# Where the stationary weights lie in their buffers: one fixed place for the seven-block chunks, eight places in turn for the plain ones

## The chip, the core and the metric

The kernel runs on one core of one Trainium2 chip. The metric is the device time of one execution in microseconds (us); a result is the median of several runs. In the profile, PE is the matrix engine (TensorE), PEld its weight loads, DVE, ACT and POOL are the vector, scalar and GpSimd engines, and SP issues most of the DMA transfers.

## What is computed

The reference is a two-layer encoder over 512 tokens of width 1024, all in float32. Layer 0 has two groups of attention heads side by side, layer 1 attention over a window of neighbours; each layer ends in a squared-ReLU network of inner width 4096. Cut to what matters here:

```python
for layer in range(DEPTH):                      # DEPTH = 2
    hn = rmsnorm(h, norm_mix[layer])
    if layer % 2 == 0:
        h = h + hybrid_attention(hn, ...)
    else:
        h = h + neighbourhood_attention(hn, w_qkv, rpb, w_out)
    hf = rmsnorm(h, norm_ffn[layer])
    u = jax.nn.relu(hf @ ffn_w_up[layer])       # 512x1024 @ 1024x4096
    h = h + (u * u) @ ffn_w_down[layer]         # 512x4096 @ 4096x1024
return rmsnorm(h, final_norm)
```

## The kernel before

**Three matmuls for one product.** Every float32 operand is held as a high part and a low part in the type `float32r`. A product of a weight block and an activation tile is three matmuls that add up in one PSUM bank: high weight with high activation, high weight with low activation, low weight with high activation. The weights are the stationary operand (a 128x128 block that PE loads before each matmul) and the activations the moving operand that streams through it.

**Weight chunks.** Weights come in chunks of up to 1024 columns. SP loads a chunk into a buffer; ACT copies it into a tile `whi` (three buffers of it), which rounds it to the high part; DVE subtracts this from the raw chunk and writes the rest to a tile `wlo` (four buffers). There are three generators for it:

- `chunk` (from L205): the plain one. ACT writes `whi` (L234, and DVE at L232 for the first), DVE writes `wlo` (L224).
- `summed_chunk` (from L248): also plain, but `wlo` is made by an ACT copy with the sign turned (L261) and a DMA that adds the raw weights to it (L263); ACT writes `whi` at L266.
- `seven_chunk` (from L362): for products that are done in seven block products instead of eight. A raw chunk holds a 2x2 arrangement of 128x128 blocks; three tensor-tensor operations, on POOL mostly (L372 to L374), make the sums and differences, ACT writes the seven blocks (896 columns) to `whi` (L379), DVE to `wlo` (L380).

A planner (`plan`, `weights`, `preload`, `begin`) keeps the list of all chunks in the order of use, loads up to five ahead and makes up to two ahead.

**The matmuls that use them.** `mm3` (L623 to L625) does the three matmuls of a plain block with moving tiles of 512 columns. `Seven.run` (L467 to L469) does the seven blocks of a seven-block chunk, three matmuls each, 21 in all, with moving tiles of 256 columns. The seven-block products stand in four runs, in each of which nothing else is on PE: 52 chunks in the first up projection, 32 in the first down projection, and 52 and 28 in the second ones: 164 chunks, 3444 matmuls. At L1728 to L1730 and L1058 to L1060 (256 columns) and L2038 to L2040 (512 columns) plain chunks are the moving operand instead.

**Places.** All activation slots and weight buffers start, in the built program, at the same remainder modulo 64 float32 columns (256 bytes), and within a slot the moving tiles start at multiples of 256 columns; the blocks of a weight tile start 128 columns apart. So what a weight tile has of its own is the number of columns from the start of its buffer, modulo 64. I call that number its **place**; place 0 is where the moving tiles lie. Before, plain chunks start at the start of their buffers and so have place 0 (but for a few blocks of other widths). Seven-block chunks go through `places()` (L355): number *i* puts its high part at column 8 (i mod 16) and its low part at a column that shifts against it every 16 chunks, so both parts go through the eight places 0, 8, 16, ... 56.

The order of the work is written out by hand; the tile framework adds the semaphores.

Of the kernel before, what the change touches and what calls it, by code (L numbers as in the profile page):

```python
# [9 lines left out]
F32R = mybir.dt.float32r  # L10
# [8 lines left out]
P = 128  # L19
# [11 lines left out]
def f32(ap):  # L31
    return ap.bitcast(F32)
# [3 lines left out]
def encoder_kernel(ctx: ExitStack, tc: tile.TileContext, ins, out, dbg=None):  # L36
# [5 lines left out]
    wp = ctx.enter_context(tc.tile_pool(name="wp", bufs=3))  # L42
# [19 lines left out]
    def nm(s):  # L62
        cnt[0] += 1
        return f"{s}_{cnt[0]}"
# [137 lines left out]
        return got[0]  # L202


    def chunk(parts, nk, ncol, heads=None, eng=None, first=False):  # L205

        raw = wp.tile([P, 1024], F32, tag="raw", bufs=4, name=nm("raw"))
        r3 = raw[:, 0 : nk * ncol].rearrange("p (k n) -> p k n", k=nk)
        for lo, n, src in parts:
            dst = r3[:, :, lo : lo + n]  # L210
            if len(src.shape) == 3:
                SP.dma_start(dst, src)
            else:
                for k in range(nk):
                    SP.dma_start(dst[:, k].rearrange("p (z m) -> p z m", z=src.shape[2]), src[:, k])
        yield
        hi = wp.tile([P, 1024], F32R, tag="whi", name=nm("whi"))
        lo_ = wp.tile([P, 1024], F32R, tag="wlo", bufs=4, name=nm("wlo"))
        m = nk * ncol
        v = lambda t: t[:, 0:m].rearrange("p (k n) -> p k n", k=nk)  # L220
        lows = []

        def low(to, src, high):
            z = lambda: (eng or DVE).tensor_tensor(to, src, f32(high), op=ALU.subtract)  # L224
            if eng:
                z()
            else:
                lows.append(z)

        if heads is None:  # L230
            if first:
                DVE.tensor_copy(hi[:, 0:m], raw[:, 0:m])  # L232
            else:
                ACT.activation(hi[:, 0:m], raw[:, 0:m], AF.Copy)  # L234
            low(lo_[:, 0:m], raw[:, 0:m], hi[:, 0:m])
        else:

            na, nb = heads
            hn = ncol // (na + nb)
            r4 = r3.rearrange("p k (h e) -> p k h e", h=hn)  # L240
            for e0, n, o in ((0, na, 0), (na, nb, hn * na)):
                z = [v(t)[:, :, o : o + hn * n].rearrange("p k (h e) -> p k h e", h=hn) for t in (hi, lo_)]
                src = r4[:, :, :, e0 : e0 + n]
                ACT.activation(z[0], src, AF.Copy)
                low(z[1], src, z[0])
        yield v(hi), v(lo_), lows

    def summed_chunk(parts, nk, ncol, heads=None, eng=None):  # L248

        raw = wp.tile([P, 1024], F32, tag="raw", bufs=4, name=nm("raw"))  # L250
        v = lambda t: t.rearrange("p (k n) -> p k n", k=nk)
        (o, n, src), = parts
        if len(src.shape) == 3:
            each = lambda t: [(v(t), src)]
        else:
            each = lambda t: [(v(t)[:, k].rearrange("p (z m) -> p z m", z=src.shape[2]), src[:, k]) for k in range(nk)]
        for d, x in each(raw):
            SP.dma_start(d, x)
        yield
        lo_ = wp.tile([P, 1024], F32R, tag="wlo", bufs=4, name=nm("wlo"))  # L260
        ACT.activation(lo_, raw, AF.Copy, scale=-1.0)  # L261
        for d, x in each(lo_):
            tc.keep_in_program_order(POOL.dma_start(d, x, accum_op=ALU.add))  # L263
        yield
        hi = wp.tile([P, 1024], F32R, tag="whi", name=nm("whi"))
        ACT.activation(hi, raw, AF.Copy)  # L266
        yield v(hi), v(lo_), []

    def rows(w, k0, nk):
        return w[k0 * P : (k0 + nk) * P, :].rearrange("(k p) n -> p k n", p=P)  # L270
# [6 lines left out]
    def plan(*spec, make=None):  # L277
        asked.append((make or chunk, spec))
        return len(asked) - 1
# [7 lines left out]
    def begin(i):  # L287
        while begun[0] < len(loaded):
            make = asked[begun[0]][0]
            if make is summed_chunk and begun[0] > i + SUM:  # L290
                break
            if make in (summed_chunk, seven_chunk):
                next(loaded[begun[0]])
            begun[0] += 1
# [55 lines left out]
    SEVEN = [(0, 0), (2, 2), (4, 5), (3, 3), (5, 4), (6, 1), (1, 6)]  # L350

    reserve = [3]
    place = [0]

    def places():  # L355

        i = place[0]
        place[0] += 1
        a = i % 16
        return 8 * a, 8 * ((a + (0, 1, 2, 4, 8, 3, 6, 12, 15, 14)[i // 16 % 10]) % 16)  # L360

    def seven_chunk(w, k0, c0, eng=None):  # L362


        slot = Slot(F32) if len(free) > reserve[0] else None
        raw = slot.t if slot else wp.tile([P, 1024], F32, tag="raw", bufs=4, name=nm("raw"))
        SP.dma_start(raw[:, 0:512].rearrange("p (k n) -> p k n", k=2), rows(w, k0, 2)[:, :, c0 : c0 + 256])
        r = raw.rearrange("p (b n) -> p b n", n=P)
        yield
        held = (lambda z: z) if eng else tc.keep_in_program_order  # L370
        eng = eng or POOL
        held(eng.tensor_tensor(r[:, 6], r[:, 0], r[:, 1], op=ALU.subtract))  # L372
        held(eng.tensor_tensor(r[:, 4:6], r[:, 2:3].to_broadcast([P, 2, P]), r[:, 0:7:6], op=ALU.add))  # L373
        held(eng.tensor_tensor(r[:, 7], r[:, 3], r[:, 5], op=ALU.subtract))  # L374
        yield
        a, b = places()
        hi = wp.tile([P, 1024], F32R, tag="whi", name=nm("whi"))[:, a : a + 896]
        lo = wp.tile([P, 1024], F32R, tag="wlo", bufs=4, name=nm("wlo"))[:, b : b + 896]
        ACT.activation(hi, raw[:, 128:1024], AF.Copy)  # L379
        DVE.tensor_tensor(lo, raw[:, 128:1024], f32(hi), op=ALU.subtract)  # L380
        if slot:
            slot.free()
        yield hi, lo, []

    class Seven:
# [63 lines left out]
        def plan(self, w, c0, pairs=None):  # L449

            return [plan(w, pairs[kp] if pairs else 2 * kp, c0, DVE if pairs and c0 and kp in (2, 5) else None,
                         make=seven_chunk)
                    for kp in range(self.np)]
# [86 lines left out]
    def product8(w, first, U, evac, eng=None):  # L540


        nk = len(U)
        ids = [plan([(0, D, rows(w, k, 1))], 1, D, None, eng, make=chunk if n < 2 else summed_chunk)
               for n, k in enumerate(first)]

# [340 lines left out]
    def load_w(k):  # L887
        w = rows(w_in, k, 1)
        W[k] = chunk([(0, 256, w[:, :, 512:768]), (256, 128, w[:, :, 0:128])], 1, 384, first=k == 0)
        next(W[k])  # L890
# [739 lines left out]
    def projC(t):  # L1630

        def ev(j, b):
# [34 lines left out]
            else:  # L1667
# [35 lines left out]
                def last():  # L1703
# [4 lines left out]
        return product(w_qkv, 0, XP, [(D * z + P * t, P) for z in range(2)], lambda j, b: ev(1 - j, b),  # L1708
                       lambda n: [mmb() for _ in range(n)], kstep=4, stride=D, order=(1, 0), nk=KD,
                       make=None if t else summed_chunk)  # L1710

    VC = {}
# [425 lines left out]
```

## Time and profile before

| what | value |
|---|---|
| median of 3 runs | 1150.22 us (1149.85 to 1150.63) |
| the profiled execution, own time | 1149.85 us |
| its span, first to last instruction | 1148.1 us |
| granted TensorE clock | 0.998 |
| PE busy | 1138.1 us, 99% of the span |
| DVE, ACT, POOL busy | 894.2, 669.3, 602.7 us |

The time of a matmul in the profile runs from its start to a modelled end and overlaps the next matmul. What counts for the time of the program is the **step**: from the start of one matmul to the start of the next. A view by windows gives it as the length of the window by the number of matmuls in it, less those that began before the window; the timeline gives it from starts, rounded to 0.01 us.

### The profile page before, as it was taken

The numbers are of one execution on the slowest core, as the hardware profiler recorded it, in microseconds if no ns is written. First come the engines' busy times: TensorE is split into PE (matmuls) and PEld (weight loads), VectorE is DVE, ScalarE is ACT, GpSimd is POOL, SyncE is SP. The second block draws the span as 40 slices with busy tenths as digits, with TensorE's granted clock in tenths as the row PEclk, the third lists the DMA queues.
The fourth block names the chain that finished last, engine by engine and source line by source line (L and its number), as shares of the span: only waits on it lengthen the run. The fifth ranks groups of instructions, "written<-read, shape, count | busy, mean of one in ns | idle before, by whom it ended". The sixth has DMA issues, their size and how long they took to land.

```text
span 1148.1 us, 20506 instructions
## 1 busy us (share of the span) xinstructions
PE 1138.1 (99%) x7348; PEld 1025.7 (89%) x7348; DVE 894.2 (78%) x1570; ACT 669.3 (58%) x1133; POOL 602.7 (52%) x722
## 2 busy tenths in 40 slices
PE   9999999999999999999999999999999999999997
PEld 8787888888899999899998998988889999989996
DVE  7887998988968777978775666667997777697874
ACT  6676785755346668534464556545553666773334
POOL 4456432327698993379432232231388889435740
PEclk9999999999999999999999999999999999999999
DMA  7322441222523235933585565333344232372332
GB/s 238 108 71 76 112 123 56 65 65 95 170 85 97 89 93 147 275 97 102 147 171 159 149 174 129 117 109 120 106 151 128 75 95 90 77 190 72 121 121 74
DMA packets 118325, 136.06 MB, mean 119 GB/s; under 512 B 9923, under 2 KB 99952, under 8 KB 118224
## 3 DMA queue, kind: packets, MB, share of 16 engines
q1 hardware_dynamic: 110736, 119.83, 34.4%
q0 software_dynamic: 7312, 14.83, 6.7%
q8 instruction: 58, 0.95, 0.4%
q14 instruction: 43, 0.35, 0.1%
q10 hardware_dynamic: 176, 0.10, 0.0%
HBM read 112.70 MB, written 6.29 MB: 104 GB/s over the span
## 4 chain that ended last, share of the span: by engine, by line
PE 92%; issue 3%; DVE 3%; ACT 1%; POOL 0%; DMA 0%; POOLq 0%; DVEq 0%; ACTq 0%
PE mm L623 9%; PE mm L624 8%; PE mm L625 8%; PE mm L468 4%; PE mm L467 4%; PE mm L469 4%; PE t L468 3%; PE t L469 3%; PE t L467 3%; PE s L1148 3%; PE o L1136 3%; PE s L467 2%; PE s L468 2%; PE s L469 2%; PE s L623 2%
## 5 line engine op out<-in xcount | busy, mean ns | idle before, releaser
L380 DVE TENSOR_TENSOR wlo<-a,whi 128x896 fp32r<-128x896 f32 x106 | 129.7, 1227 | 58.9 <-ACT whi L379 58.4
L623 PE MATMUL mm<-a,whi 128*128 128x512 f32 x428 | 172.7, 404 | 0.1
L624 PE MATMUL mm<-a,whi 128*128 128x512 f32 x428 | 167.9, 392 | 0.0
L625 PE MATMUL mm<-a,wlo 128*128 128x512 f32 x428 | 167.0, 391 | 0.0
L379 ACT ACTIVATE whi<-a 128x896 fp32r<-128x896 f32 x106 | 100.8, 951 | 111.8 <-PE s L468 28.5
L224 DVE TENSOR_TENSOR wlo<-raw,whi 128x1024 fp32r<-128x1024 f32 (+4 forms) x93 | 105.4, 1139 | 27.0 <-ACT whi L234 26.6
L234 ACT ACTIVATE whi<-raw 128x1024 fp32r<-128x1024 f32 (+3 forms) x96 | 88.2, 920 | 56.3 <-PE s L624 23.2
L468 PE MATMUL mm<-a,whi 128*128 128x256 f32 x430 | 120.8, 281 | 0.0
L469 PE MATMUL mm<-a,wlo 128*128 128x256 f32 x430 | 120.7, 281 | 0.0
L467 PE MATMUL mm<-a,whi 128*128 128x256 f32 x430 | 120.6, 281 | 0.0
L379 ACT ACTIVATE whi<-raw 128x896 fp32r<-128x896 f32 x58 | 55.1, 954 | 84.1 <-PE s L468 23.0
L373 POOL TENSOR_TENSOR a<-a 128x256 f32<-128x256 f32 x104 | 96.9, 932 | 8.2
L625 PEld LDWEIGHTS mm<-a,wlo 128*128 128x128 f32 x428 | 80.3, 188 | 17.1
L374 POOL TENSOR_TENSOR a<-a 128x128 f32<-128x128 f32 x104 | 90.5, 870 | 8.2
L1156 POOL TENSOR_SCALAR p<-p,ti 128x512 f32<-128x512 f32 x64 | 48.0, 751 | 88.4 <-DVE ti L1155 67.7
L623 PEld LDWEIGHTS mm<-a,whi 128*128 128x128 f32 x428 | 80.5, 188 | 15.5 <-issue 0.5
L624 PEld LDWEIGHTS mm<-a,whi 128*128 128x128 f32 x428 | 80.7, 189 | 13.5
L372 POOL TENSOR_TENSOR a<-a 128x128 f32<-128x128 f32 x104 | 77.2, 743 | 27.8 <-DMA a<-in_ffn_w_up_dram 23.1
L1785 POOL TENSOR_SCALAR p<-p,ti 128x256 f32<-128x256 f32 x64 | 35.6, 567 | 104.5 <-DVE ti L1784 91.6
L380 DVE TENSOR_TENSOR wlo<-raw,whi 128x896 fp32r<-128x896 f32 x58 | 71.0, 1235 | 24.6 <-ACT whi L379 24.5
L468 PE MATMUL t<-a,whi 128*128 128x256 f32 x312 | 87.5, 281 | 0.0
L469 PE MATMUL t<-a,wlo 128*128 128x256 f32 x312 | 87.5, 280 | 0.0
(449 smaller groups left out, 3618.8 us busy)
## 6 DMA issues: line engine op xcount, KB each, us to landing
a<-in_ffn_w_up_dram SPq DMA_DIRECT2D x102, 256.0 KB, 2.7
raw<-in_ffn_w_down_dram SPq DMA_DIRECT2D x34, 512.0 KB, 4.4
raw<-in_ffn_w_down_dram SPq DMA_DIRECT2D x56, 256.0 KB, 2.6
raw<-in_od_w_qkv_dram SPq DMA_DIRECT2D x64, 128.0 KB, 3.5
raw<-in_ffn_w_up_dram SPq DMA_DIRECT2D x12, 512.0 KB, 4.1
wlo<-in_ffn_w_down_dram POOLq DMA_DIRECT2D x12, 512.0 KB, 6.2
a<-a SPq DMA_DIRECT2D x17, 256.0 KB, 3.4
bx<-a SPq DMA_DIRECT2D x32, 128.0 KB, 5.4
```

The source lines that it names most:

```text
L224: z = lambda: (eng or DVE).tensor_tensor(to, src, f32(high), op=ALU.subtract)
L234: ACT.activation(hi[:, 0:m], raw[:, 0:m], AF.Copy)
L373: held(eng.tensor_tensor(r[:, 4:6], r[:, 2:3].to_broadcast([P, 2, P]), r[:, 0:7:6], op=ALU.add))
L374: held(eng.tensor_tensor(r[:, 7], r[:, 3], r[:, 5], op=ALU.subtract))
L379: ACT.activation(hi, raw[:, 128:1024], AF.Copy)
L380: DVE.tensor_tensor(lo, raw[:, 128:1024], f32(hi), op=ALU.subtract)
L467: PE.matmul(o, wh, x[:, 0], start=kp == 0 and n in (0, 1, 3, 5), stop=False, skip_group_check=True)
L468: PE.matmul(o, wh, x[:, 1], start=False, stop=False, skip_group_check=True)
L469: PE.matmul(o, wl, x[:, 0], start=False, stop=kp == self.np - 1, skip_group_check=True)
L623: PE.matmul(o, wh, xh, start=first, stop=False)
L624: PE.matmul(o, wh, xl, start=False, stop=False)
L625: PE.matmul(o, wl, xh, start=False, stop=last)
```

## The change

Seven-block chunks all get one place: both parts start at column 16 of their buffers. Plain chunks, of both generators, now go through `places()`: chunk *i* has its high part at column 8 (i mod 8) and its low part at 8 ((i mod 8 + i div 8) mod 8), so that every pair of the eight places 0 to 56 occurs in turn. To make room, `whi` and `wlo` buffers are 1088 columns wide instead of 1024 (a multiple of 64 again, so a place means the same as before). The order of the instructions on every engine, their sizes and what they wait for are the same as before.

```diff
+    place = [0]
+    def places():
+        i = place[0]
+        place[0] += 1
+        a = i % 8
+        return 8 * a, 8 * ((a + i // 8) % 8)
     def chunk(parts, nk, ncol, heads=None, eng=None, first=False):
...
-        hi = wp.tile([P, 1024], F32R, tag="whi", name=nm("whi"))
-        lo_ = wp.tile([P, 1024], F32R, tag="wlo", bufs=4, name=nm("wlo"))
+        a, b = places()
+        hi = wp.tile([P, 1088], F32R, tag="whi", name=nm("whi"))[:, a : a + 1024]
+        lo_ = wp.tile([P, 1088], F32R, tag="wlo", bufs=4, name=nm("wlo"))[:, b : b + 1024]
...
     def summed_chunk(parts, nk, ncol, heads=None, eng=None):
...
-        lo_ = wp.tile([P, 1024], F32R, tag="wlo", bufs=4, name=nm("wlo"))
+        a, b = places()
+        lo_ = wp.tile([P, 1088], F32R, tag="wlo", bufs=4, name=nm("wlo"))[:, b : b + 1024]
...
-        hi = wp.tile([P, 1024], F32R, tag="whi", name=nm("whi"))
+        hi = wp.tile([P, 1088], F32R, tag="whi", name=nm("whi"))[:, a : a + 1024]
...
-    place = [0]
-    def places():
-        i = place[0]
-        place[0] += 1
-        a = i % 16
-        return 8 * a, 8 * ((a + (0, 1, 2, 4, 8, 3, 6, 12, 15, 14)[i // 16 % 10]) % 16)
     def seven_chunk(w, k0, c0, eng=None):
...
-        a, b = places()
-        hi = wp.tile([P, 1024], F32R, tag="whi", name=nm("whi"))[:, a : a + 896]
-        lo = wp.tile([P, 1024], F32R, tag="wlo", bufs=4, name=nm("wlo"))[:, b : b + 896]
+        hi = wp.tile([P, 1088], F32R, tag="whi", name=nm("whi"))[:, 16:912]
+        lo = wp.tile([P, 1088], F32R, tag="wlo", bufs=4, name=nm("wlo"))[:, 16:912]
```

## The prediction

> **What bounds the kernel now.** I read the page's busy table and its chain first, then what PE waited for, then the matmuls' pace in the four runs of seven-block chunks.
>
> ```profile
> span 1148.1 us, 20506 instructions
> PE 1138.1 (99%) x7348; PEld 1025.7 (89%) x7348; DVE 894.2 (78%) x1570; ACT 669.3 (58%) x1133; POOL 602.7 (52%) x722
> PE 92%; issue 3%; DVE 3%; ACT 1%; POOL 0%; DMA 0%; POOLq 0%; DVEq 0%; ACTq 0%
> ```
>
> PE is busy for 99% of the span and the chain that ended last lies on it. The longest entry in the list of what PE waited for, and one of the shortest:
>
> ```profile
> PE o L158 <- POOL zeros L131: 1.0, 1, 1.0
> PE t L652 <- DVE rsB L722: 0.2, 1, 0.2
> ```
>
> So no wait is there to be won. The order of the instructions is unchanged, and the only way for this edit to move the time is the step from one matmul to the next. The windows view, one window inside each of the four seven-block runs (length, PE busy, number of matmuls):
>
> ```profile
> 319.00:447.00 128.00, 128.00 (x1086) 128.00 (x1086) 94.13 (x109) 83.04 (x104) 107.42 (x128) 1.00 0.29 86
> ...
> 491.00:570.00 79.00, 79.00 (x670) 79.00 (x669) 59.40 (x70) 33.97 (x40) 58.37 (x64) 1.00 0.36 116
> ...
> 873.00:1001.00 128.00, 128.00 (x1085) 128.00 (x1085) 93.78 (x108) 82.52 (x103) 106.71 (x127) 1.00 0.28 83
> ...
> 1046.00:1114.00 68.00, 68.00 (x578) 68.00 (x577) 53.50 (x65) 27.57 (x32) 44.22 (x50) 1.00 0.39 125
> ```
>
> A matmul here lasts 281 ns by the groups below, so each window also counts the 2.4 that began before it: 403 us / (3419 - 9.5) = **118.2 ns a step**. The whole-span windows view of L467 and of L624 gives their counts, 1148 and 703; times three, 3444 seven-block and 2109 plain matmuls:
>
> ```profile
> 0.00:1149.00 1149.00, 321.92 (x1148) 1.00 0.42 118
> ```
> ```profile
> 0.00:1149.00 1149.00, 274.84 (x703) 1.00 0.42 118
> ```
>
> **The seven-block chunks.** Before, they went through all places, so the trace already holds the place that they all get now. First and last of the 21 matmuls of four chunks, 20 steps between them: chunk 6 (both parts at column 48), chunk 10 (both at 80, which is place 16), chunk 64 (columns 0 and 64, place 0), chunk 66 (16 and 80, place 16).
>
> ```profile
> 333.38 0.28 PE L467 MATMUL s<-a,whi 128*128 128x256 f32 x1
> ...
> 335.73 0.28 PE L469 MATMUL o<-a,wlo 128*128 128x256 f32 x1
> ```
> ```profile
> 343.32 0.28 PE L467 MATMUL mm<-a,whi 128*128 128x256 f32 x1
> ...
> 345.59 0.28 PE L469 MATMUL s<-a,wlo 128*128 128x256 f32 x1
> ```
> ```profile
> 520.75 0.28 PE L467 MATMUL mm<-a,whi 128*128 128x256 f32 x1
> ...
> 523.14 0.28 PE L469 MATMUL s<-a,wlo 128*128 128x256 f32 x1
> ```
> ```profile
> 525.74 0.28 PE L467 MATMUL mm<-a,whi 128*128 128x256 f32 x1
> ...
> 528.01 0.28 PE L469 MATMUL s<-a,wlo 128*128 128x256 f32 x1
> ```
>
> 2.35 us / 20 = 117.5 ns; 2.27 / 20 = **113.5**; 2.39 / 20 = 119.5; 113.5 again. There are five chunks with both parts at place 16 (numbers 2, 10, 66, 74 and 162: the first up projection and both down projections are among them), and each takes this pace from its first matmul to its last; no chunk at another pair of places holds it throughout. The same shows in the mean time of a matmul: the page's group of L467, and the group of L467 inside chunk 10 alone.
>
> ```profile
> L467 PE MATMUL mm<-a,whi 128*128 128x256 f32 x430 | 120.6, 281 | 0.0
> ```
> ```profile
> L467 PE MATMUL mm<-a,whi 128*128 128x256 f32 x5 | 1.4, 276 | 0.0
> ```
>
> Since the wider buffers are again multiples of 64 columns, the change gives all 164 chunks these places: (118.2 - 113.5) x 3444 = **-16.2 us**, all of it on PE and so on the path. Bounds: -16.2 if all four runs fall into this pace, -2.4 (0.7 ns x 3444) if all keep the 117.5 of chunk 6. I take the full value: a run that has it is not disturbed, because no other matmul stands within a run and all chunks now have one place, while the five chunks of before had neighbours at other places and took the pace at once.
>
> One rule speaks against this. The Trainium skill, "SBUF — State Buffer", section "Who interferes with whom", gives PE a read port for the moving operand and an independent one for weight loads, and says that PE never waits on anyone. By it the place of a weight tile would not matter and the sum would be 1150. The rows of chunks 64 and 66, one after the other with the same instructions and 6 ns apart in the step, differ from it.
>
> **The plain chunks.** They leave place 0 and go through all pairs of places. The rows show place 0 alone. In the down projections, where 24 matmuls of a chunk follow each other undisturbed, its step is (all PE, two windows):
>
> ```profile
> 449.00:490.00 41.00, 41.00 (x182) 1.00 0.93 261
> 1004.00:1044.00 40.00, 40.00 (x179) 1.00 0.59 152
> ```
>
> With 1.7 matmuls of 389 ns begun before each, 81 us / 357.6 = 226.5 ns. This is twice 113.3, the undisturbed pace for twice the columns: place 0 is a good one for 512 columns once the pattern has settled. It is not always settled. Where other matmuls come between, the step is longer for some matmuls; a stretch of six at the same place 0:
>
> ```profile
> 50.06 0.39 PE L624 MATMUL mm<-a,whi 128*128 128x512 f32 x1
> ...
> 51.45 0.39 PE L624 MATMUL mm<-a,whi 128*128 128x512 f32 x1
> ```
>
> 1.39 us / 6 = 231.7 ns. Over all plain chunks the mean matmul of L624 lasts 274.84 / 703 = 391.0 ns, against 389 in the settled window:
>
> ```profile
> L624 PE MATMUL mm<-a,whi 128*128 128x512 f32 x15 | 5.8, 389 | 0.0
> ```
>
> so the mean step before is about 228.5. At other places, bounds from these rows: all 2109 settled, -2.0 ns or -4.2 us; none settled, +3.2 ns or +6.7 us; 6 ns above the settled step, as chunk 64 has it against chunk 66, 232.5 or +8.4 us. With 256 columns only one pair of places in 64 was seen to hold the best pace throughout, and a chunk of 24 matmuls has a new pair each time, so I take three quarters of the way to "none settled": **+5.0 us**.
>
> Where plain chunks are the moving operand (L1728 to L1730, 128 matmuls each), the mean is at place 0
>
> ```profile
> 0.00:1149.00 1149.00, 36.21 (x128) 1.00 0.42 118
> ```
>
> 282.9 ns for L1729, and the mean of L467 over all places is 321.92 / 1148 = 280.4. Taking that for the new mixture: 2.5 x 384 = **-1.0 us**; at best 276, -2.6; at worst nothing.
>
> The copies on ACT and DVE write to shifted columns. Seven-block chunks were shifted before as well; I cost it at nothing, and PE's lead hides it.
>
> **Do the others keep up?** PE would ask for a chunk 21 x 4.7 = 0.1 us earlier each time, 5.1 us over 52 chunks. POOL's sums are the slowest supplier:
>
> ```profile
> L373 POOL TENSOR_TENSOR a<-a 128x256 f32<-128x256 f32 x104 | 96.9, 932 | 8.2
> L374 POOL TENSOR_TENSOR a<-a 128x128 f32<-128x128 f32 x104 | 90.5, 870 | 8.2
> L372 POOL TENSOR_TENSOR a<-a 128x128 f32<-128x128 f32 x104 | 77.2, 743 | 27.8 <-DMA a<-in_ffn_w_up_dram 23.1
> ```
>
> 2.55 us a chunk against 21 x 113.5 = 2.38 us on PE. It lives on a head start. Last sum and first matmul of chunk 4, and of chunk 51, the run's last:
>
> ```profile
> 301.54 0.79 POOL L374 TENSOR_TENSOR a<-a 128x128 f32<-128x128 f32 x1
> ```
> ```profile
> 328.38 0.28 PE L467 MATMUL s<-a,whi 128*128 128x256 f32 x1
> ```
> ```profile
> 434.28 1.32 POOL L374 TENSOR_TENSOR a<-a 128x128 f32<-128x128 f32 x1
> ```
> ```profile
> 444.91 0.28 PE L467 MATMUL mm<-a,whi 128*128 128x256 f32 x1
> ```
>
> The lead falls from 26.0 us to 9.3. With PE 5.1 us earlier 4.2 remain, and ACT's and DVE's copies need 951 and 1227 ns:
>
> ```profile
> L379 ACT ACTIVATE whi<-a 128x896 fp32r<-128x896 f32 x106 | 100.8, 951 | 111.8 <-PE s L468 28.5
> L380 DVE TENSOR_TENSOR wlo<-a,whi 128x896 fp32r<-128x896 f32 x106 | 129.7, 1227 | 58.9 <-ACT whi L379 58.4
> ```
>
> 2.2 us of 4.2: it holds, narrowly. ACT itself is released by PE freeing `whi`, which will come earlier.
>
> **The rivals.**
> - *A run sticks in another pattern.* Chunk 6 shows a steady 117.5. One run of 52 chunks stuck there gives back 1092 x 4.0 = 4.4 us, all four 13.8. For it: the same places may have two patterns, and a run starts from other matmuls. Against: five of five. One or two runs: 1142 to 1146. Chance 0.14.
> - *POOL becomes the bound at the end of the up projections.* The lead ends up used if ACT's other work (evacuations of 0.6 to 1 us) delays a copy by 2 us; some 2 us in each up projection, 1142. Chance 0.08.
> - *Plain chunks settle in a bad pattern*, +8.4 or a little over: 1141 to 1145. Chance 0.08.
> - *Places do nothing* (the page's rule; seen as mere coincidence in the rows): 1150. Chance 0.02.
> - *Slower:* the runs settle in the pattern of chunk 64, as they may if the distance to the neighbouring chunk and not the place itself made the five chunks fast. Then 1.3 x 3444 = +4.5 with +5.0 - 1.0: 1158. It decides once the seven-block step stays above 118.2 - 4.0 us / 3444 = 117.0 ns. Chance 0.03.
>
> **How the numbers follow.** From the profiled execution's own 1149.85 us (span 1148.1 and 1.75 around it; 0.37 below the median): -16.2 + 5.0 - 1.0 = 1137.65, with 0.37 for the median **1138.0**. Chance of this case 0.65. Its own range is 1133 (plain chunks at no loss, -16.2 - 1.0) to 1141.5 (at +8.4); the first three rivals carry the upper end to 1145, and what lies below 1133 needs plain chunks that gain. Anything beyond 0.2% (2.3 us) counts as a difference, about what a measurement of this kernel can tell from none. Faster 0.94: the forecast and the first three rivals, less 0.01 for all four runs stuck; same 0.03; slower 0.03.
>
> **What would show it.** Right: in the windows of the four runs a step of 113.5 ns (128 us would hold about 1130 matmuls), L467's group at 276 or 277 ns, the down-projection windows of plain chunks above 226.5, L624's mean above 391. PE still without waits; POOL's lead at the end of the first up projection near 4 us. Wrong: a seven-block group still at 280, a run at 117.5, PE waiting for `whi` or `wlo` late in an up projection, or plain matmuls longer than 396 ns in the mean.

## The result, and the profile after

| | before | after |
|---|---|---|
| median | 1150.03 us (4 runs, 1149.38 to 1150.63) | 1156.16 us (4 runs, 1155.08 to 1156.93) |
| ratio, 95% interval | | 1.0054 [1.0041, 1.0066] |
| span of the profiled execution | 1148.1 us | 1155.2 us |

The kernel became 0.5% slower, where 1138 us had been forecast. PE's share is 99% as before:

```profile
span 1155.2 us, 20506 instructions
PE 1143.2 (99%) x7348; PEld 1022.8 (89%) x7348; DVE 896.9 (78%) x1570; ACT 668.4 (58%) x1133; POOL 591.8 (51%) x722
```

So the steps have to tell it. The windows view of the matmuls alone, with windows laid inside the four seven-block runs (the second and the fourth in two pieces each) and, last, inside the two stretches of plain chunks of the down projections; the columns are window, its length, PE busy and number of matmuls, granted clock, DMA share, GB/s:

```profile
322.00:448.00 126.00, 126.00 (x1072) 1.00 0.29 84
494.00:513.00 19.00, 19.00 (x170) 1.00 0.33 106
525.00:572.00 47.00, 47.00 (x401) 1.00 0.36 118
879.00:1006.00 127.00, 127.00 (x1081) 1.00 0.28 82
1052.00:1088.00 36.00, 36.00 (x320) 1.00 0.39 123
1101.00:1119.00 18.00, 18.00 (x155) 1.00 0.45 145
453.00:492.00 39.00, 39.00 (x169) 1.00 0.95 265
1009.00:1048.00 39.00, 39.00 (x170) 1.00 0.59 152
```

Taking off the 2.4 matmuls that began before each window (1.7 for the plain ones), the steps are 117.8, **113.4**, 117.9, 117.7, **113.4**, 118.0 ns, and 232.4 ns (78 us / 335.6) for the plain chunks, which had 226.5. All seven-block chunks now have one place, and yet there are two paces and nothing between. The first and the third run never had the fast one; the second and the fourth began with it and lost it. What PE waited for there is new, first in the fourth run, then in the second:

```profile
PE s L470 <- DVE wlo L381: 1.8, 1, 1.8
...
PE mm L470 <- DVE wlo L381: 0.3, 1, 0.3
```

The timeline of PE at the longer of the two, late in the fourth run:

```profile
1090.87 0.28 PE L468 MATMUL s<-a,whi 128*128 128x256 f32 x1
1090.98 0.28 PE L469 MATMUL s<-a,whi 128*128 128x256 f32 x1
1093.04 0.39 PE L470 MATMUL s<-a,wlo 128*128 128x256 f32 x1 [1.78 <-DVE wlo L381]
1093.26 0.28 PE L468 MATMUL t<-a,whi 128*128 128x256 f32 x1
1093.38 0.28 PE L469 MATMUL t<-a,whi 128*128 128x256 f32 x1
...
1093.85 0.28 PE L470 MATMUL t<-a,wlo 128*128 128x256 f32 x1
1093.96 0.28 PE L468 MATMUL t<-a,whi 128*128 128x256 f32 x1
```

and of DVE, which had the missing `wlo` (L381) in its queue behind block sums whose load had not landed and behind the evacuation of the group before:

```profile
1087.86 0.83 DVE L374 TENSOR_TENSOR raw<-raw 128x128 f32<-128x128 f32 x1 [1.26 <-DMA raw<-in_ffn_w_down_dram]
1088.61 0.67 DVE L480 TENSOR_TENSOR a<-a,s 128x512 f32<-128x512 f32 x1
1089.21 0.64 DVE L375 TENSOR_TENSOR raw<-raw 128x256 f32<-128x256 f32 x1
1089.77 1.75 DVE L1603 TENSOR_TENSOR hT<-hT,a 128x1024 f32<-128x1024 f32 x1
1091.45 0.54 DVE L376 TENSOR_TENSOR raw<-raw 128x128 f32<-128x128 f32 x1
1091.91 3.08 DVE L381 TENSOR_TENSOR wlo<-raw,whi 128x896 fp32r<-128x896 f32 x3
```

The wait costs more than its length. Before it the step is 113 ns (0.11 us as the starts are rounded); after it one step is 220 ns, the next four are about 120, and then it is 113 again. But then, in a windows view of the matmuls, the granted clock (the number behind the count of matmuls) halves for 3.4 us:

```profile
1093.00:1094.30 1.30, 1.26 (x10) 1.00 0.16 24
1094.30:1097.70 3.40, 3.40 (x18) 0.50 0.70 221
1097.70:1100.00 2.30, 2.30 (x22) 1.00 0.14 42
```

The pattern of 117.8 ns stands from the end of this stretch on. So in the fourth run the fast pattern outlived the wait and was gone after the half clock; in the second run it was gone right after a wait of 0.3 us, with the clock at 1.00.

Where the 7.1 us of the spans came from, as sums over the starts of matmuls in the two traces: the 2109 plain steps took 490.9 us and take 498.3 (**+7.4**); the 3444 seven-block steps took 406.9 and take 407.2 (**+0.3**: by an estimate, the 588 steps of the 28 chunks at 113.4 ns won 2.8 us against the mean before, the stretches at 117.8 some 1.0, and the waits and the half clock ate some 4.1); the 432 steps with weights as the moving operand of 256 columns took 52.7 and take 52.1 (**-0.6**).

### The profile page after: what moved, and what is told of

It reads as the page before. It is cut to its first block, busy times and chain, and to the rows that moved or that the text cites. A ratio compares the mean times of both kernels' runs of the same rounds, so it can differ in the third digit from the quotient of the medians.

```text
span 1155.2 us, 20506 instructions
## 1 busy us (share of the span) xinstructions
PE 1143.2 (99%) x7348; PEld 1022.8 (89%) x7348; DVE 896.9 (78%) x1570; ACT 668.4 (58%) x1133; POOL 591.8 (51%) x722
## 4 chain that ended last, share of the span: by engine, by line
PE 91%; issue 4%; DVE 2%; POOL 1%; ACT 1%; DMA 0%; POOLq 0%; DVEq 0%; ACTq 0%
PE mm L624 9%; PE mm L626 9%; PE mm L625 9%; PE mm L470 4%; PE mm L468 4%; PE mm L469 4%; PE s L1149 3%; PE t L470 3%; PE t L468 3%; PE t L469 3%; PE o L1137 3%; PE s L624 2%; PE s L625 2%; PE s L626 2%; PE s L470 2%
## 5 line engine op out<-in xcount | busy, mean ns | idle before, releaser
L381 DVE TENSOR_TENSOR wlo<-a,whi 128x896 fp32r<-128x896 f32 x106 | 131.1, 1239 | 57.9 <-ACT whi L380 57.7
L624 PE MATMUL mm<-a,whi 128*128 128x512 f32 x428 | 174.0, 407 | 0.1
L625 PE MATMUL mm<-a,whi 128*128 128x512 f32 x428 | 168.9, 395 | 0.0
L376 POOL TENSOR_TENSOR a<-a 128x128 f32<-128x128 f32 x104 | 98.7, 949 | 8.1
L375 POOL TENSOR_TENSOR a<-a 128x256 f32<-128x256 f32 x104 | 94.0, 904 | 8.2
L624 PEld LDWEIGHTS mm<-a,whi 128*128 128x128 f32 x428 | 80.6, 188 | 16.1 <-issue 0.5
L625 PEld LDWEIGHTS mm<-a,whi 128*128 128x128 f32 x428 | 80.7, 189 | 14.6
L381 DVE TENSOR_TENSOR wlo<-raw,whi 128x896 fp32r<-128x896 f32 x58 | 69.4, 1213 | 25.3 <-ACT whi L380 25.2
L468 PE MATMUL t<-a,whi 128*128 128x256 f32 x312 | 87.7, 281 | 0.0
L469 PE MATMUL t<-a,whi 128*128 128x256 f32 x312 | 87.7, 281 | 0.0
```

The source lines that it names most:

```text
L468: PE.matmul(o, wh, x[:, 0], start=kp == 0 and n in (0, 1, 3, 5), stop=False, skip_group_check=True)
L469: PE.matmul(o, wh, x[:, 1], start=False, stop=False, skip_group_check=True)
L624: PE.matmul(o, wh, xh, start=first, stop=False)
L625: PE.matmul(o, wh, xl, start=False, stop=False)
```

## The experiments

The theory after the result: place 16 has two patterns that hold themselves, 113.4 and 117.8 ns. What stands before a run decides which one it gets, a wait of PE can change it, and the fast one is faster than the down projections can be fed; the plain chunks lose because, of the places tried, 512 columns settle at 226.7 ns at place 0 alone. The rivals are named in the expectations. Every kernel was compared with runs of the kernel before on the same chip.

**Plain chunks back at place 0** (e1; seven-block chunks at 16 as in the change):

```diff
-        return 8 * a, 8 * ((a + i // 8) % 8)
+        return 0, 0
```

> Plain chunks back at place 0, seven-block chunks all at place 16 as in the changed kernel. Theory (place 16 has two self-holding patterns, 113.4 and 117.8 ns a step, and what stands before a run or a wait decides which one holds; the spread places of the plain chunks cost 7.4 us): plain steps back to 228.2 ns, seven-block stretches at either 113.4 or 117.8 and nothing between, about 1149 us if they fall as in the changed kernel, 1134 if all hold 113.4. Rival A (the plain places are harmless and place 16 is what costs): it stays at 1156. Rival B (nothing but the neighbour's place makes a chunk fast): all seven-block steps at 117.8.

1148.13 us, ratio 0.9983 [0.9974, 0.9993]; span 1145.6. Windows in the first run, in two pieces of the second, in the third, the fourth, and in plain chunks:

```profile
320.00:446.00 126.00, 126.00 (x1073) 1.00 0.30 83
492.00:509.00 17.00, 17.00 (x146) 1.00 0.34 109
522.00:554.00 32.00, 32.00 (x285) 1.00 0.32 99
872.00:998.00 126.00, 126.00 (x1073) 1.00 0.28 82
1044.00:1111.00 67.00, 67.00 (x572) 1.00 0.40 126
450.00:489.00 39.00, 39.00 (x174) 1.00 0.96 270
```

117.7, 118.4, **113.2**, 117.7, 117.6, and 226.3 ns for the plain ones. The plain term is won back, and with it the whole loss: this kernel is 1.7 us faster than the one before. Rival A falls. The second and fourth run now begin slow, with nothing changed in them but what stands before. By the starts of matmuls in the second run, a pause of 0.1 us left it slow, one of 0.3 us made it fast, and one of 0.06 us made it slow again. So the place alone does not decide, and a wait works both ways.

**The seven-block chunks rotating as before, the plain ones spread as in the change** (e2):

```diff
+        a = i % 16
+        a, b = 8 * a, 8 * ((a + (0, 1, 2, 4, 8, 3, 6, 12, 15, 14)[i // 16 % 10]) % 16)
-        hi = wp.tile(...)[:, 16:912]
-        lo = wp.tile(...)[:, 16:912]
+        hi = wp.tile(...)[:, a : a + 896]
+        lo = wp.tile(...)[:, b : b + 896]
```

> Seven-block chunks rotate through the places as before, plain chunks spread as in the changed kernel. Theory: the plain steps rise to 232 ns as they did, the seven-block steps stay at 118.1, so 1150 + 7.4 = 1157.5 us. Rival A: 1150.

1157.07 us, ratio 1.0066 [1.0049, 1.0083], as the theory had it. Windows in the first run and in plain chunks:

```profile
322.00:448.00 126.00, 126.00 (x1070) 1.00 0.29 84
453.00:492.00 39.00, 39.00 (x170) 1.00 0.97 266
```

118.0 and 231.7 ns. The spread places of the plain chunks are the whole loss by themselves.

**Two lead-in chunks** (e3). Plain chunks at place 0; in each run the first chunk at place 0, the second at 8, the others at 16:

```diff
+        i -= max(n for n in (0, 52, 84, 136) if n <= i)
+        a = b = 8 * min(i, 2)
```

> Plain chunks at place 0; in each of the four runs the first seven-block chunk is at place 0, the second at place 8, all others at place 16, so that each run begins as the five fast chunks of before were led in to. Theory (entry decides, the pattern then holds itself): the first run holds 113.4 ns from its third chunk, the others too if the lead-in is what matters, until PE has to wait; 1150 - 16 plus what is lost after waits, 1135 to 1146 us. Rival B (a chunk is fast only right after one at place 8): one fast chunk in each run, 117.8 after it, 1149.

1141.53 us, ratio 0.9933 [0.9918, 0.9948]. Windows in two pieces of the first run, in the third, and in the fourth:

```profile
324.00:356.00 32.00, 32.00 (x285) 1.00 0.28 83
364.00:444.00 80.00, 80.00 (x681) 1.00 0.31 87
916.00:990.00 74.00, 74.00 (x655) 1.00 0.31 90
1040.00:1078.00 38.00, 38.00 (x336) 1.00 0.38 119
```

113.2, then 117.9 after two short pauses (0.2 and 0.1 us) of which the second cost it the pattern, 113.4, 113.9. All four runs have 113.3 to 113.4 ns in their third chunk. In the third run two chunks of 52 changed against e1, and from there to its end the step is 4.4 ns shorter: the entry decides, and the pattern holds itself. Rival B falls. In the fourth run the fast pattern outlived a wait of 2.3 us and 3.4 us at half the clock, so a wait need not end it.

**High part at 16, low part at 48** for all seven-block chunks, plain at 0 (e4):

```diff
+        a, b = 16, 48
```

> Plain chunks at place 0; all seven-block chunks with the high part at place 16 and the low part at place 48, the pair at which four chunks of before came from a wandering step into 113.4 ns after some 13 matmuls. Theory (a pair of places whose only lasting pattern is the fast one gets it from any entry and again after a wait): 113.4 ns in all four runs but for some 15 matmuls after each entry and wait, 1136 to 1142 us, the rest being waits for DVE. Rival C (the fast pattern is an accident of each entry at any pair): some runs fast, some not, 1143 to 1150.

1141.80 us, ratio 0.9932 [0.9915, 0.9949]. Two windows in the first run, on both sides of waits, and one in the second:

```profile
320.00:357.00 37.00, 37.00 (x329) 1.00 0.28 83
370.00:395.00 25.00, 25.00 (x223) 1.00 0.34 98
490.00:550.00 60.00, 60.00 (x530) 1.00 0.35 109
```

113.3, 113.3, 113.7: at this pair all four runs have the fast pattern from their second chunk on by themselves, and get it back after every wait. Rival C falls. In time it only equals the lead-in: its seven-block steps took 400.2 us, where 113.3 ns throughout would be 390.3. The longest of the waits, in the down projections:

```profile
PE mm L476 <- DVE wlo L387: 2.6, 1, 2.6
PE s L476 <- DVE wlo L387: 1.2, 2, 1.0
```

The rest of the 9.9 us went in pauses too short for this list, in the up projections too (3.5 us), and in 3.4 us at half the clock. The traces of e3 and e4 are of the longest of four executions each (1144.06 and 1144.57 us), so not every execution loses as much.

**Less of the block sums on DVE in the down projections** (three kernels, each as the one with 16 and 48):

```diff
-  DVE if pairs and c0 and kp in (2, 5) else None
+  DVE if pairs and c0 and kp == 2 else None     # e5
+  None                                          # e6
+  DVE if pairs and c0 and kp == 5 else None     # e8
```

> As e4 (plain chunks at place 0, seven-block chunks at 16 and 48), but in the down projections DVE makes the block sums of one chunk in eight (pair 2) instead of two (pairs 2 and 5), POOL the others. Theory (with the fast pattern the feed is the bound: in e4 PE waited 2.6 us late in the first down projection and 1.0 us in the second for wlo, which stood on DVE behind the sums of pair 5 and their load, and then ran 3.4 us at half the clock): these waits go, 1136 to 1138 us. Rival (POOL, with 2.55 us a chunk against 2.38 on PE, becomes the bound): 1141 or more, with waits for ACT copies that wait for POOL.

> As e4, but POOL makes the sums of all chunks. Theory: the two long waits for wlo behind DVE's sums go as in e5, but POOL now needs 2.55 us for every chunk against 2.38 on PE, so over 28 to 32 chunks it falls some 5 us behind, of which its head start of 4 to 10 us takes most: 1136 to 1142 us. Rival: it is POOL that was late in e4 as well; then it is slower than e4's 1141.8 by 3 us or more.

> As e5, but DVE keeps the sums of pair 5 and gives those of pair 2 to POOL. Theory: the long waits of e4 come late in a group of chunks, where pair 5's sums and the evacuation of the group before stand ahead of a wlo on DVE; so here they stay, about 1140 to 1142 us, against 1136 to 1138 in e5. Rival (any relief of DVE helps alike): the same time as e5.

1143.49 (ratio 0.9936 [0.9919, 0.9953]), 1145.60 (0.9960 [0.9945, 0.9974]) and 1145.77 us (0.9958 [0.9942, 0.9974]): none is better than 1141.80, and all three forecasts were missed. What PE waited for with pair 2 alone on DVE:

```profile
PE mm L476 <- DVE wlo L387: 2.9, 4, 1.5
PE s L476 <- DVE wlo L387: 0.8, 2, 0.7
```

The one long wait became several shorter ones of the same total. POOL now has the sums that DVE gave up, and what DVE and ACT waited for in the first down projection (window 488 to 566 us) shows it, first in e4, then in e6:

```profile
DVE wlo L387 <- ACT whi L386: 10.8, 7, 2.5
...
ACT whi L386 <- POOL raw L381: 17.9, 11, 2.5
```
```profile
DVE wlo L387 <- ACT whi L386: 29.0, 21, 2.4
...
ACT whi L386 <- POOL raw L381: 31.2, 20, 1.8
```

That fits the rivals of e5 and e6, in their times too. Since the edit takes work from one supplier and gives it to another, it can't tell which of the two bounded e4; this stays open. In e8 the long wait stayed, as forecast (3.7 us), but the time was 3.8 us above the forecast's upper end.

**One place other than 0 for all plain chunks** (e7; seven-block ones at 16 and 48):

```diff
-        return 0, 0
+        return 16, 16
```

> As e4, but all plain chunks have both parts at place 16 instead of 0: one place for all, so no change from chunk to chunk. Theory (place 0 is the one at which matmuls of 512 columns settle): plain steps of 231 to 234 ns as with the spread places, 1141.8 + 7 = 1149 us. Rival (what costs is that the place changes from chunk to chunk): plain steps of 227 to 229 ns again, 1142.

1148.81 us, ratio 0.9995 [0.9985, 1.0005], 7.0 us above the same kernel with plain chunks at 0. Window in plain chunks:

```profile
450.00:490.00 40.00, 40.00 (x173) 1.00 0.93 263
```

233.5 ns. With one place for all chunks it is no better than with the spread ones: the place costs, not its change from chunk to chunk. By the starts, in the down projections every stretch of 24 matmuls steps by 233.3 ns here, by 226.7 at place 0, and with the spread places by 230.3 to 235.5; of the places other than 0 only 16 was tried alone.

**A longer lead** (e9, e9b, e11). Four `whi` buffers and chunks made three ahead; the room comes from buffers back at 1024 columns and one scratch buffer less (e9), or one probability tile less (e9b); e11 is e9 with rotating places:

```diff
-    hi = wp.tile([P, 1088], F32R, tag="whi", name=nm("whi"))
+    hi = wp.tile([P, 1024], F32R, tag="whi", bufs=4, name=nm("whi"))
-    AHEAD, SUM, LOAD = 2, 3, 5
+    AHEAD, SUM, LOAD = 3, 3, 5
-    scp: bufs=6                # e9; e9b: pp: bufs=5
+    scp: bufs=5                # e9; e9b: pp: bufs=4
```

> As e4 (plain chunks at place 0, seven-block chunks at 16 and 48), with four whi buffers instead of three, chunks made three ahead instead of two, and one scratch buffer less (five) to make room. Theory (in the fast pattern PE is short of weights only because DVE's blocks of evacuations are longer than the 2.5 us by which wlo is ahead): wlo is some 2.4 us further ahead, the waits in the down projections and the half clock after them go, 1134 to 1138 us. Rival (throughput of POOL, DVE or the loads is the bound, not the lead): waits of the same length later in each run, 1140 to 1143.

> As e9, but the room comes from the pool of probability tiles (four instead of five) and the scratch buffers stay at six. Theory: the same gain in the seven-block runs as e9, 1134 to 1138 us, unless the attention stages need the fifth tile. Rival as in e9.

> The buffers and the lead of e9, but seven-block chunks rotate through the places as before and plain chunks are at place 0: tells what the buffers do by themselves. Theory (at 118.1 ns a step PE never waits, so a longer lead has nothing to remove): 1150 us. Rival (the buffers or the order of the work bring a gain of their own): 1147 or less.

1142.13 (0.9934 [0.9919, 0.9949]), **1138.40** (0.9902 [0.9885, 0.9918]) and 1154.42 us (1.0042 [1.0027, 1.0057]). The two up projections of e9b, nearly whole, and the waits left in the down projections:

```profile
320.00:442.00 122.00, 122.00 (x1079) 1.00 0.30 83
870.00:992.00 122.00, 122.00 (x1079) 1.00 0.31 84
```
```profile
PE o L474 <- DVE hT L1566: 1.3, 1, 1.3
...
PE mm L476 <- DVE wlo L387: 0.8, 2, 0.5
...
PE s L476 <- DVE wlo L387: 0.5, 1, 0.5
```

113.3 ns without a break through both up projections, as in e9: there the lead, or the fourth buffer, was what lacked. e9b came out just above its forecast and e9 at the time that its rival gave, but without the rival's sign: its longest wait for `wlo` was 1.3 us, against 2.6 in e4. In the down projections shorter waits remain. The rotating kernel (e11), forecast at 1150, shows that lead and buffers bring nothing at 118 ns: with one scratch buffer less it is 0.4% slower than before. e9 and e9b differ in the buffer given up alone, and by 3.7 us, so the missing scratch buffer is the likely price in both e9 and e11; where it is paid was not tested by itself. Neither the lead nor the fourth buffer was tried alone.

**Fast places in the up projections alone** (e10):

```diff
+        if i < 52 or 84 <= i < 136:
+            return 16, 48
```

> Places 16 and 48 in the two runs of 52 chunks (up projections) alone; the down projections rotate through the places as before, plain chunks at place 0. Theory (the fast pattern gains some 3.9 us in each up projection, and what it gains in the down projections is given back in waits for wlo): 1150 - 8 = 1142 us, the same as e4. Rival (the down projections have their share of e4's gain): 1145 to 1146.

1142.96 us, ratio 0.9942 [0.9927, 0.9956], 1.2 us from e4 at two runs of 52 chunks instead of all: nearly all of e4's gain is made in the up projections. By the starts in e4's trace, the up projections took 251.1 us against 258.0 before, the down projections 149.1 against 148.9: with three buffers, what the fast pattern gains there is given back in waits.

## Why the prediction was wrong

- **The step that failed: "a run that has it is not disturbed ... the five chunks of before had neighbours at other places and took the pace at once", from which all 164 chunks were given 113.5 ns.** That each of the five "takes this pace from its first matmul to its last" was read rightly. But the five fast chunks (2, 10, 66, 74, 162) were one case seen five times: by the rule of `places()` each had a chunk with both parts at place 8 before it. A rotation through places gives every place much the same predecessor, so five of five said nothing about other entries. The lead-in experiment shows that this entry leads to the fast pattern, in four runs of four; without it two runs in four (changed kernel) and none in four (plain at 0) began fast. In the changed kernel 28 of 164 chunks had the fast pace, nearly all others 117.8 ns, and of the two runs that began with it one lost it at a wait, the other by the end of the half clock that followed a wait. The term of -16.2 us measured +0.3 with its waits.
- **The rival of the sticking pattern** had the right mechanism and nearly the right pace (117.5 forecast, 117.8 measured); it was priced at 13.8 us for all four runs, but "all four stuck" was given 0.01.
- **The feed** was looked for in the wrong place. POOL's head start in the up projections was not used up: at the last chunk of the first one 10.7 us were left in the changed kernel, where PE was slow in that run, and 6.7 in e4, where it was fast (4.2 forecast). PE waited in the down projections, up to 1.8 us, for a `wlo` that was late on DVE, whose queue was not costed: the `wlo` before it was written one chunk (2.4 us) ahead of PE, and then DVE was taken up from 1088.61 to 1091.91 us with other work. That a wait can also end the pattern, and that a long one is followed by 3.4 us at half the clock, was in no term.
- **Plain chunks:** that leaving place 0 costs was right, the size too small: +5.0 forecast, +7.4 measured. The reason given for "three quarters of the way" to "none settled", a new pair with each chunk, is not what the runs show: at one fixed place 16 (e7) the step is as long. It should have been all of the way, +6.7, and a little more: the mean of L625 (L624 before) went from 391.0 to 394.5 ns, by 277.35 us in 703 matmuls:

```profile
0.00:1156.00 1156.00, 277.35 (x703) 1.00 0.41 118
```

- **Weights as the moving operand:** -1.0 forecast, -0.6 measured.
- The rule on independent read ports (the Trainium skill, "SBUF — State Buffer", section "Who interferes with whom"), as the prediction reads it, would have left the time at 1150. The traces do not agree with it: 226.3 ns at place 0 (e1) and 233.5 at place 16 (e7), with the same instructions.

With -16.2 replaced by +0.3, +5.0 by +7.4 and -1.0 by -0.6, the forecast's sum is 1149.85 + 7.1 = 1156.95, the time of the profiled execution (1156.93). The three terms are measured in the two traces, so this shows that nothing else moved, not that their causes are known.

## What to carry to other kernels

A natural experiment inside a trace, here a rotation of places, shows a state together with the way into it: before a term rests on "it always does so there", ask whether all the cases had the same history, and try it from another. Before the bound engine is made 4% faster, look through the queue of every supplier for blocks longer than its lead, and price what a wait sets off and not the wait alone. Keep the good half of a change: the fixed pair of places with more lead, and plain weights left at place 0, is 1% faster than the kernel that it started from.

## What the runs showed of the hardware

- The step of back-to-back matmuls depends on the column at which the stationary blocks start, with the moving tiles left where they are: from 113.3 to 120 ns in the mean of a chunk at 256 moving columns, 226.7 ns at place 0 and 233.3 at place 16 at 512. Columns 16 and 80 behave alike in chunks 2, 10 and 66, which is why places are counted modulo 64. The pattern that holds is not always a function of the place: at 16 and 16 there are two.
- The steady steps by the starts of matmuls are 17, 34 and 35 times 6.67 ns (113.3, 226.7 and 233.3); that of 117.8 is not a multiple, but three of it are 53 times 6.67. That may mean a slot of this length that the matmuls lock to. No run tested it, and what in the memory or the engine makes the patterns stays open.
- In the traces, a wait of PE of 1.78 us or more (1.78, 2.29, 2.31, 2.59 and 3.72 in five kernels) was followed within about 1.3 us by 3.4 us at a granted clock of 0.50, each time; waits of up to 1.47 us were not. In the kernel with 16 and 48, a windows view after its 2.6 us wait:

```profile
556.50:558.00 1.50, 1.50 (x9) 0.50 0.77 202
```
